# An encoder layer on one core: the first weights' fetch, two weight sums and one mean put elsewhere in the order

## The chip, the cores and the metric

The kernel runs on one core of a Trainium2 chip. The metric is the device time of one launch in microseconds (us). The engines are PE (TensorE: matmuls and transposes; PEld is its weight load), DVE (VectorE), ACT (ScalarE), POOL (GpSimd) and SP (SyncE, which here only issues DMA transfers). ACT and POOL also have DMA queues of their own. A line number such as L844 is a line of the kernel before.

## The reference

One encoder layer over x (1024 tokens, width 1024) with a conditioning vector c. It has three residual sub-layers, each `x <- LayerNorm(ALPHA * x + w * gate(c) * f(x * (1 + scale(c)) + shift(c)))`: a SwiGLU feed-forward network with a hidden width of 2816, a mixer (half convolution with 31 taps, half differential attention with 4 heads of two softmax maps each), and a second feed-forward network. Scale, shift and gate are products of silu(c) with a matrix of 1024 x 9216.

```python
def swiglu(h, w_in, w_out):
    gate, up = jnp.split(h @ w_in, 2, axis=-1)
    return (jax.nn.silu(gate) * up) @ w_out
```

## The kernel before, in words

Every fp32 operand is split into a rounded part and its remainder (`split`, L142: the cast on ACT at L143, the subtraction on DVE at L144), and a product takes three matmuls: high x high, high x low, low x high. The feed-forward networks multiply by a Strassen-like scheme with seven products: weights and activations are cut in quarters, and sums of quarters are formed on DVE (`in_sums`, L359, for the weights; the `t` tiles in `mid` for the activations).

The input phase of a feed-forward network works on 22 pairs j of column strips, one gate and one up strip each. `in_load` (L336) fetches a pair's raw weights in four transfers of 256 KB, `in_gate` (L352) splits the gate's quarters into `ah` and `al`, and `in_sums` forms four sums (L364 to L366, L368) and splits them into `sh` and `sl`.

The startup of the first network is written out by hand in `early` (L818). It works through four blocks kk of 256 columns. `first_ada` (L756) and `first_x` (L767) issue the loads on SP. `first_mod` (L773) multiplies the conditioning matrix by silu(c), partly on DVE (L780, L782), partly on PE (L788), and joins the halves on PE (L798) and ACT (`part` at L795, B and A at L802). `first_h` transposes x on PE (L810), and ACT applies B and A (`h`, L280). The result is rounded on ACT (L845), and `right_lo` (L830) forms its remainder on DVE (L832). The first pair's raw weights are issued on ACT's queue at the very start; its gate split stands behind block 0, the first three sums and their split behind block 1, the fourth behind block 3.

`mid` (L859) then treats the second half of the tokens: `h`, the sums `t` (L876, L877) with their splits, and behind the first products the subtractions of L899 and L900. From there `in_steps` (L411) runs the pairs, and `hook(j)` (L945) puts other work between them: `mix_load` (L919) and `mix_part` (L925) fetch parts of the mixer's weights on POOL's DMA queue, two per pair, split them and store them to a scratch in memory.

`out_phase` (L558) is the second half of a feed-forward network: 7 x 11 steps, each with its `prep` (L572: loads on SP, splits) and 12 matmuls (L610); `evac` (L626) takes the results out. In the first network's output phase, between the steps, `sums_load` (L668) fetches pieces of the second network's weights on POOL's queue, and `sums_part` (L675) forms their sums, splits them and stores them (L686). There are eight such units, one every nine steps. The same stretch runs the layer norm of finished tokens (`rstd_of`, L240, a power on POOL at L244; `nm` at L259; the scaling on ACT at L260).

In the attention, `scores` (L1183) makes two score maps per step, with a row-max on DVE (L1196) and an exponential on ACT. Beside it `conv_flip` and `conv_stat` (L1308) do the convolution's layer norm over channels: variances, a power on POOL (L1313), the negative scaled means `nm` (L1317, DVE), a scaling on ACT (L1320). `conv_back` (L1323) transposes the result back.

The order on each engine is that of a planner, which starts from the order of the program. `tc.issue_after(x)` ties an instruction behind x, on x's own engine alone. `pace["V"]` and `pace["S"]` hold the latest marked instructions of DVE and ACT.

## Time and profile before

| | |
|---|---|
| median of 3 runs | 1866.86 us (1865.17 to 1867.88) |
| profiled execution | 1868.7 us |
| its span | 1866.9 us |
| PE busy | 97% |
| DVE busy | 77% |
| ACT busy | 42% |
| POOL busy | 17% |
| DMA, mean | 160 GB/s |

The span is what the profile's times count from, first instruction to last; the execution's own time is 1.8 us longer. Busy shares are over the whole span. A time in brackets at the end of a row is how long the engine was idle ahead of the instruction, and what it then waited for.

### The profile page before, as it was taken

The numbers are of one execution on the slowest core, as the hardware profiler recorded it, in microseconds if no ns is written. First come the engines' busy times: TensorE is split into PE (matmuls) and PEld (weight loads), VectorE is DVE, ScalarE is ACT, GpSimd is POOL, SyncE is SP. The second block draws the span as 40 slices with busy tenths as digits, with TensorE's granted clock in tenths as the row PEclk, the third lists the DMA queues.
The fourth block names the chain that finished last, engine by engine and source line by source line (L and its number), as shares of the span: only waits on it lengthen the run. The fifth ranks groups of instructions, "written<-read, shape, count | busy, mean of one in ns | idle before, by whom it ended". The sixth has DMA issues, their size and how long they took to land.

```text
span 1866.9 us, 23501 instructions
## 1 busy us (share of the span) xinstructions
PE 1808.8 (97%) x8538; PEld 1499.9 (80%) x8538; DVE 1440.4 (77%) x2029; ACT 784.7 (42%) x1296; POOL 308.7 (17%) x336
## 2 busy tenths in 40 slices
PE   4999999999999999999999999999999999999997
PEld 4788888887888877888888888878888888888886
DVE  6988787898699788899876676587775766569888
ACT  3633333333455543112167783363333333354540
POOL 0001010011211122026658650100000000000011
PEclk9999999999999999999999999999999999999999
DMA  9378777775895423322100027145553443187432
GB/s 318 105 232 289 248 236 232 248 266 185 290 360 178 147 68 119 107 68 78 59 1 1 24 91 248 70 143 188 174 177 119 138 131 127 52 300 273 130 119 74
DMA packets 223602, 299.22 MB, mean 160 GB/s; under 512 B 16618, under 2 KB 127327, under 8 KB 223486
## 3 DMA queue, kind: packets, MB, share of 16 engines
q1 hardware_dynamic: 207018, 249.44, 41.2%
q0 software_dynamic: 13120, 45.10, 6.8%
q10 hardware_dynamic: 3348, 3.18, 0.5%
q8 instruction: 67, 1.10, 0.2%
q14 instruction: 49, 0.40, 0.1%
HBM read 215.35 MB, written 82.31 MB: 159 GB/s over the span
## 4 chain that ended last, share of the span: by engine, by line
PE 70%; DVE 12%; DMA 6%; ACT 4%; POOL 3%; issue 3%; SPq 1%; POOLq 0%; DVEq 0%; ACTq 0%
PE fo L610 16%; PE glu L1046 4%; PE mo L1428 4%; PE vp L1093 2%; PE kp L1093 2%; ACT p L1198 2%; PE fi_4A L396 1%; PE fi_9A L396 1%; PE fi_6A L396 1%; PE fi_14A L396 1%; PE fi_10A L396 1%; PE fi_16A L396 1%; PE fi_11A L396 1%; PE fi_8A L396 1%; PE qp L1093 1%
## 5 line engine op out<-in xcount | busy, mean ns | idle before, releaser
L610 PE MATMUL fo<-wr,gl 128*128 128x512 f32 x1848 | 422.3, 390 | 3.9 <-DVE pv L653 2.5
L610 PEld LDWEIGHTS fo<-wr,gl 128*128 128x128 f32 x1848 | 346.2, 188 | 78.0 <-DVE pv L653 3.7
L1065 DVE SCALAR_TENSOR_TENSOR cacc<-u,convw,cacc 128x1012 f32<-128x1012 f32 (+14 forms) x120 | 151.0, 1325 | 0.2
L144 DVE TENSOR_TENSOR gl<-gr,gl 128x512 fp32r<-128x512 f32 x148 | 101.9, 694 | 11.6 <-ACT gl L143 10.1
L143 ACT CAST gl<-gr 128x512 fp32r<-128x512 f32 x148 | 90.9, 618 | 31.3 <-DMA gr<-gd 25.4
L144 DVE TENSOR_TENSOR sl<-sf,sh 128x1024 fp32r<-128x1024 f32 x40 | 49.0, 1224 | 65.0 <-ACT sh L143 64.9
L1196 DVE TENSOR_REDUCE mx<-sc 128x1 f32<-128x1024 f32 x64 | 75.5, 1216 | 25.4 <-PE sc L1194 25.3
L1198 ACT ACTIVATE p<-sc,mx 128x1024 f32<-128x1024 f32 x64 | 71.3, 1115 | 35.7 <-DVE mx L1196 35.6
L143 ACT CAST sh<-sf 128x1024 fp32r<-128x1024 f32 x40 | 42.2, 1054 | 103.0 <-issue 7.9
L156 DVE SCALAR_TENSOR_TENSOR ada<-adaw,c_act,ada 128x512 f32<-128x512 f32 x98 | 73.3, 748 | 13.1 <-DMA adaw<-in_w_ada_dram 12.8
L418 POOL DMA_DIRECT2D gd<-gf x8 | 4.3, 542 | 430.9 <-DVE gf L484 429.7
L244 POOL TENSOR_TENSOR rr<-rv,mhalf 128x1 f32<-128x1 f32 x24 | 22.1, 920 | 290.7 <-DVE rv L242 290.6
L446 ACT ACTIVATE gf<-gf 128x512 f32<-128x512 f32 x44 | 27.8, 633 | 96.4 <-DVE gf L445 96.3
L466 ACT ACTIVATE gf<-gf 128x512 f32<-128x512 f32 x44 | 27.7, 629 | 96.2 <-DVE gf L465 96.2
L143 ACT CAST wr<-wa 128x512 fp32r<-128x512 f32 x66 | 41.1, 623 | 59.3 <-PE fo L610 55.6
L144 DVE TENSOR_TENSOR sl<-r,sh 128x1024 fp32r<-128x1024 f32 x44 | 53.6, 1222 | 16.0 <-ACT sh L143 15.7
L1046 PE MATMUL glu<-hm,gluh 128*128 128x512 f32 x256 | 65.6, 392 | 0.0
L1247 POOL TENSOR_TENSOR p<-p,p 128x1024 f32<-128x1024 f32 x27 | 64.2, 2376 | 1.5
L143 ACT CAST wr<-wb 128x512 fp32r<-128x512 f32 x66 | 40.1, 620 | 56.5 <-PE fo L610 36.7
L1264 PE MATMUL av<-vf,aT 128*128 128x128 f32 x512 | 62.4, 276 | 0.8 <-ACT cacc L1327 0.8
L144 DVE TENSOR_TENSOR wr<-wa,wr 128x512 fp32r<-128x512 f32 x66 | 45.5, 690 | 19.9 <-ACT wr L143 19.9
L1264 PEld LDWEIGHTS av<-vf,aT 128*128 128x128 f32 x512 | 59.8, 192 | 1.3 <-ACT cacc L1327 1.1
(3439 smaller groups left out, 4853.2 us busy)
## 6 DMA issues: line engine op xcount, KB each, us to landing
gr<-gd SPq DMA_DIRECT2D x148, 256.0 KB
adaw<-in_w_ada_dram SPq DMA_DIRECT2D x56, 512.0 KB
gd<-gf SPq DMA_DIRECT2D x102, 256.0 KB
r<-in_ffn_w_in_dram SPq DMA_DIRECT2D x84, 256.0 KB
ra<-in_ffn_w_in_dram SPq DMA_DIRECT2D x66, 256.0 KB
mwi<-mw POOLq DMA_DIRECT2D x24, 512.0 KB, 5.5
wb<-in_ffn_w_out_dram SPq DMA_DIRECT2D x44, 256.0 KB
wa<-in_ffn_w_out_dram SPq DMA_DIRECT2D x44, 256.0 KB
```

The source lines that it names most:

```text
L143: a = S.copy(hi, x)
L144: b = eng.tensor_tensor(lo, x, hi.bitcast(F32), ALU.subtract)
L156: V.scalar_tensor_tensor(acc, raw[:, jj], c_act[:, n : n + 1], acc, ALU.mult, ALU.add)
L396: pe_last[:] = [PE.matmul(ps, lhsT=w[:, k], rhs=x, start=k == 0 and n == 0 and not more, stop=k == 3 and n == 2, skip_group_check=more,).ins]
L610: PE.matmul(ps, lhsT=g[:, x, ts_], rhs=w[:, y], start=n in (1, 2, 3) and k == i == 0, stop=k == NK - 1 and i == 2, skip_group_check=n not ...
L1046: PE.matmul(q[2 * m + h], lhsT=w[:, m * P : (m + 1) * P], rhs=hm[k][h][:, x], start=k == 0 and n == 0, stop=k == KD - 1 and n == 2,)
L1065: V.scalar_tensor_tensor(acc[:, lo_t:hi_t], u[:, lo_t + sh : hi_t + sh], convw[:, i, jj : jj + 1], acc[:, lo_t:hi_t], ALU.mult, ALU.add,)
L1093: PE.matmul(pss[t], lhsT=hk[:, x, ts_], rhs=w, start=k == 0 and n == 0, stop=k == KD - 1 and n == 2)
L1196: V.tensor_reduce(mx_, ps, axis=AX.X, op=ALU.max, negate=True)
L1198: S.activation(pe, ps, AF.Exp, bias=mx_, accum_out=sm[:, e : e + 1])
L1264: PE.matmul(ps[:, 0:P], lhsT=aT[:, kt], rhs=vf[kt][:, h * P : (h + 1) * P], start=kt == 0, stop=kt == 7)
L1428: pe = PE.matmul(ps, lhsT=x[:, ts_], rhs=w[:, ds_], start=n == 0, stop=n == total - 1)
```

## The change

Four edits. In `early`, the first pair's raw weights are issued behind the second block's rounding on ACT, and the gate split, the four sums and their splits stand behind the last block. In `mid`, the subtractions of L899 and L900 stand behind the last remainder of the `t` tiles. Two of the eight weight sums leave the output phase and are done by `mix_load` and `mix_part` as the last two units, behind the 40 units of the mixer's weights. In the attention, `nm` of `conv_stat` stands behind the latest row-max.

```diff
@@ out_phase
-            if s == 0 and i < 72:
-                if i % 9 == 2:
-                    ms = sums_load(i // 36, i // 9 % 4)
-                elif i % 9 == 8:
-                    sums_part(ms, i // 36, i // 9 % 4)
+            if s == 0 and i < 54:
+                n_, at = divmod(i, 9)
+                if at == 2:
+                    ms = sums_load(*divmod(n_ + 2, 4))
+                elif at == 8:
+                    sums_part(ms, *divmod(n_ + 2, 4))
@@ early
-            with tc.issue_after(c_silu.ins):
-                raws = [in_load(wp, s, w_in, 0, S)]
+            raws = [None]
...
                     rounded = S.copy(hi[kk], hb[kk]).ins
+                if kk == 1:
+                    with tc.issue_after(rounded):
+                        raws[0] = in_load(wp, s, w_in, 0, S)
                 with tc.issue_after(summed):
                     if kk:
                         right_lo(kk - 1)
-                    if kk == 0:
+                    if kk == 3:
                         L[0].update(in_gate(wp, s, 0, raws[0]))
-                    elif kk == 1:
-                        in_sums(wp, s, 0, raws[0], L[0], order=(0,))
-                    elif kk == 3:
-                        right_lo(3)
-                        in_sums(wp, s, 0, raws[0], L[0], order=(1,))
+                        ra, rb, r4 = raws[0]
+                        V.tensor_tensor(ra[:, 2], rb, ra[:, 2], ALU.add)
+                        V.tensor_tensor(rb, ra[:, 0], rb, ALU.subtract)
+                        V.tensor_tensor(ra[:, 0], ra[:, 2], ra[:, 0], ALU.subtract)
+                        V.tensor_tensor(ra[:, 1], ra[:, 1], ra[:, 0], ALU.subtract)
+                        for i in range(2):
+                            sh = wp.tile([P, 2, 4, P], F32R, tag="sh", bufs=3, name=f"sh{s}_0_{i}")
+                            sl = wp.tile([P, 2, 4, P], F32R, tag="sl", bufs=3, name=f"sl{s}_0_{i}")
+                            with tc.issue_after(rounded):
+                                split(sh, sl, r4[:, i::2])
+                            L[0].update({f"S{2 * i + 2 - e}": (sh[:, e], sl[:, e]) for e in range(2)})
+                            if i == 0:
+                                right_lo(3)
@@ mid
+            ready = rest
             for kk in range(5):
                 if kk < 4:
                     b, h, t = hb[kk], hc[kk], t12[kk]
-                    right_b22(f"r0_{kk}", ops, h)
-                    V.tensor_tensor(h[:, 0], h[:, 1], h[:, 0], ALU.subtract)
-                    V.tensor_tensor(h[:, 1], b[:, 1], t[:, 1], ALU.subtract)
+                    with tc.issue_after(ready):
+                        right_b22(f"r0_{kk}", ops, h)
+                        V.tensor_tensor(h[:, 0], h[:, 1], h[:, 0], ALU.subtract)
+                        V.tensor_tensor(h[:, 1], b[:, 1], t[:, 1], ALU.subtract)
@@ mix_load, mix_part, units
+            if isinstance(src, tuple):
+                r = t[:, 0].rearrange("p (s n) -> p s n", s=4)
+                for dst, x in zip((r[:, 0::3], r[:, 1:3]), src):
+                    G.dma_start(dst, x)
+            else:
+                G.dma_start(t[:, 0], src)
...
-                if hs:
+                if hs and hs[0] is None:
+                    sums_of(t[:, 0].rearrange("p (s n) -> p s n", s=4))
+                elif hs:
...
+            if hs and hs[0] is None:
+                for x in range(2):
+                    G.dma_start(dst[:, x], t[:, x].rearrange("p (s n) -> p s n", s=4))
+            else:
+                G.dma_start(dst, t)
...
+        w2 = a["ffn2_w_in"][0].rearrange("(k e p) (s n) -> k e p s n", e=2, p=P, s=2)
+        for k in range(2):
+            units.append((tuple(w2[k, e][:, :, 0:P] for e in range(2)), mws[0][:, :, :, k], None))
@@ scores
-                V.tensor_reduce(mx_, ps, axis=AX.X, op=ALU.max, negate=True)
+                pace["V"] = V.tensor_reduce(mx_, ps, axis=AX.X, op=ALU.max, negate=True).ins
@@ conv_stat
-            V.scalar_tensor_tensor(nm, mv[:, :, 0], -1.0, r, ALU.mult, ALU.mult)
+            with tc.issue_after(pace["V"]):
+                V.scalar_tensor_tensor(nm, mv[:, :, 0], -1.0, r, ALU.mult, ALU.mult)
```

`sums_of` holds the same four sums as L679 to L682.

## Rows read from the trace of the kernel before

**Rows 1.** The page's first part: busy us, share, instructions of each engine.
```profile
PE 1808.8 (97%) x8538; PEld 1499.9 (80%) x8538; DVE 1440.4 (77%) x2029; ACT 784.7 (42%) x1296; POOL 308.7 (17%) x336
```

**Rows 2.** Stretches: length, busy PE, PEld, DVE, ACT, POOL, PE's clock, DMA share, GB/s.
```profile
14.00:40.00 26.00, 16.51 (x75) 15.66 (x75) 19.25 (x25) 11.09 (x33) 0.00 (x0) 1.00 1.09 347
50.00:67.00 17.00, 17.00 (x86) 14.00 (x85) 16.89 (x22) 13.98 (x19) 0.00 (x0) 1.00 0.22 62
67.00:83.00 16.00, 14.17 (x58) 9.98 (x57) 15.34 (x21) 9.91 (x13) 0.00 (x0) 1.00 0.20 64
1056.00:1060.00 4.00, 3.62 (x14) 2.95 (x15) 1.51 (x5) 4.00 (x11) 2.68 (x2) 0.50 0.00 0
```

**Rows 3.** The chain of waits up to 85 us: start, length, what.
```profile
20.63 6.76 DMA ada<-in_w_ada_dram
...
27.41 6.76 DMA ada<-in_w_ada_dram
...
41.22 5.67 DMA xc<-in_x_dram
```

**Rows 4.** Timeline of the DMA triggers on ACT's and SP's queues, startup.
```profile
3.13 6.83 ACTq L349 DMA_DIRECT2D r<-in_ffn_w_in_dram  x3
...
35.11 6.07 SPq L349 DMA_DIRECT2D r<-in_ffn_w_in_dram  x4
...
52.03 2.02 SPq L349 DMA_DIRECT2D r<-in_ffn_w_in_dram  x4
```

**Rows 5.** Timeline of ACT, startup.
```profile
15.42 1.47 ACT L143 CAST ah<-r 128x1536 fp32r<-128x1536 f32 x1 [12.50 <-DMA r<-in_ffn_w_in_dram]
...
29.92 1.05 ACT L143 CAST sh<-r 128x1024 fp32r<-128x1024 f32 x1
30.86 1.06 ACT L845 CAST r_1bh<-h 128x1024 fp32r<-128x1024 f32 x1
31.80 0.73 ACT L795 ACTIVATE part<-ada0q,bada 128x1 f32<-128x1 f32 x4
39.36 0.41 ACT L802 ACTIVATE B<-ada0p,part 128x1 f32<-128x1 f32 x2 [6.83 <-PE ada0p L798]
...
39.96 1.46 ACT L280 ACTIVATE h<-hT,B,A 128x512 f32<-128x512 f32 x2
```

**Rows 6.** Timeline of DVE, startup.
```profile
16.92 1.76 DVE L144 TENSOR_TENSOR al<-r,ah 128x1536 fp32r<-128x1536 f32 x1 [1.43 <-ACT ah L143]
...
25.24 0.69 DVE L366 TENSOR_TENSOR r<-r 128x512 f32<-128x512 f32 x1
...
49.59 1.23 DVE L832 TENSOR_TENSOR r_3bl<-h,r_3bh 128x1024 fp32r<-128x1024 f32 x1 [4.25 <-ACT r_3bh L845]
50.73 1.22 DVE L144 TENSOR_TENSOR sl<-r,sh 128x1024 fp32r<-128x1024 f32 x1
```

**Rows 7.** Timeline of the first output phase, 660 to 692 us, all engines.
```profile
662.84 0.77 POOL L686 DMA_DIRECT2D mws<-ms  x1 [2.29 <-issue]
...
664.23 0.21 DVE L259 TENSOR_SCALAR nm<-mv,rr 128x1 f32<-128x1 f32 x1 [2.82 <-POOL rr L244]
...
668.21 3.04 PE L610 MATMUL fo<-wr,gl 128*128 128x512 f32 x12 [1.55 <-DVE pv L653]
...
683.10 0.29 DVE L680 TENSOR_TENSOR ms<-ms 128x128 f32<-128x128 f32 x1
...
689.65 2.59 PE L610 MATMUL fo<-wr,gl 128*128 128x512 f32 x10 [0.93 <-DVE wr L144]
```

**Rows 8.** Timeline of DVE, 498 to 512 us.
```profile
504.24 0.69 DVE L144 TENSOR_TENSOR wr<-wb,wr 128x512 fp32r<-128x512 f32 x1 [2.49 <-ACT wr L143]
```

**Rows 9.** Timeline of the attention: DVE and PE at 1053 to 1117 us.
```profile
1052.90 0.16 DVE L1317 SCALAR_TENSOR_TENSOR cnm<-cmv,cr 128x4 f32<-128x4 f32 x1 [4.37 <-POOL cr L1313]
...
1055.98 0.73 PE L1178 MATMUL qTl<-ident_r,ql 128*128 128x128 f32 x4 [2.34 <-DVE aT L1256]
...
1116.87 1.91 PE L276 MATMUL cB<-ident,cacc 128*128 128x128 f32 x16
```

More of the change, by code (lines that the diff above doesn't have):

```diff
@@ L921, in mix_load, with sums_of @@
             t = wp.tile([P, 2, H], F32, tag="mw", bufs=2, name="mw")
-            G.dma_start(t[:, 0], src)
-            loaded.append((t, *rest))
+            if isinstance(src, tuple):
[4 more added lines that the diff above has]
+                G.dma_start(t[:, 0], src)
+            loaded.append((t, *rest))
+        def sums_of(r):
+            V.tensor_tensor(r[:, 2], r[:, 3], r[:, 2], ALU.add)
+            V.tensor_tensor(r[:, 3], r[:, 0], r[:, 3], ALU.subtract)
+            V.tensor_tensor(r[:, 0], r[:, 2], r[:, 0], ALU.subtract)
+            V.tensor_tensor(r[:, 1], r[:, 1], r[:, 0], ALU.subtract)
         def mix_part():
@@ L932, in mix_part @@
                 V.tensor_tensor(t[:, 0].bitcast(F32R), t[:, 0], t[:, 1], ALU.subtract)
-            G.dma_start(dst, t)
+            if hs and hs[0] is None:
[3 more added lines that the diff above has]
+                G.dma_start(dst, t)
         units = []
```

## The prediction, made before the changed kernel ran

> **What bounds the kernel now.** I read the page's list of engines first: PE is busy for 97% of the 1866.9 us [rows 1], so all that an edit can win are the few stretches in which PE stands or runs at half clock; an edit that fills idle time of another engine is worth nothing. The table by stretches then gives the stages. Startup, 14 to 40 us: the DMA engines are full (share 1.09, 347 GB/s) while DVE has 19.25 of 26 us and ACT 11.09. At 50 to 67 us, where the first pair's products run, DVE has 16.89 of 17 us and PE 17.00; at 67 to 83 DVE has 15.34 of 16 and PE only 14.17 [rows 2]. So until 83 us DVE is nearly solid: what comes late on DVE at 50 us comes late for PE too. The chain of waits up to 85 us shows why the startup lasts as long as it does: transfer after transfer, each link beginning where the one before ended (20.63 + 6.76 = 27.39, then 27.41) [rows 3]. Between two links lie eight transfers in the order of the program, those of SP and ACT counted together: I read it as eight counters used in turn, where a transfer is issued only when the one eight before it has landed. That reading carries my largest term.
>
> **Part 1, the first pair's raw weights (`early`).** Removed from the start: four transfers of 256 KB, 1.05 MB, which at 347 GB/s [rows 2] held up all later ones by 3.0 us. They now stand on ACT behind the second block's rounding, in program order behind all 46 others of the startup.
>
> When does ACT get there? That rounding is at 30.86 for 1.06 us [rows 5], so 31.92; it is 3.0 earlier by the bytes, and the first `sh` cast (1.05, at 29.92 [rows 5]) no longer stands ahead of it: 27.9.
>
> When may it issue? Before, the block transfer whose link begins at 27.41 lands at 34.17 [rows 3]. Behind it are five more of these (1.31 MB), three x pieces (0.52 MB each) and the second pair's four raw pieces; at that rate they land at 37.9, then 39.4, 40.9, 42.4, then 43.2, 43.9. After the change all is 3.0 earlier. The eight counters make the moved four wait for the last two x pieces and the first two raw ones: 37.9, 39.4, 40.2, and about 42 for the last, which by then shares the engines. ACT executes in order, so it stands at its triggers from 27.9 to about 42.4. The last lands a link later, 5.67 by the shortest late link [rows 3]: 47.4 (a link is 5.67 to 6.76).
>
> What is queued behind ACT's triggers: the third block's `part` (0.73 [rows 5]), its B, A and `h` (39.36 to 41.42, 2.1 [rows 5]). From 42.4 that gives 45.2. Then the gate cast `ah`, which now needs the landing: 47.4 + 1.47 [rows 5] = 48.9; third rounding 49.9; fourth `part` 0.7, B, A, `h` 2.1, rounding 1.06: 53.8. DVE: third remainder 51.1, `al` 1.76, sums 4 x 0.69, fourth remainder 1.23 and two `sl` of 1.22 less their overlap [rows 6]: 52.9, 55.6, 56.8, 58.5. Before, DVE was through with the second `sl` at 51.95 [rows 6]. So it is 6.5 late, and in a stage where DVE is solid PE is late by about as much; PE's 1.83 us of idle time at 67 to 83 [rows 2] takes back perhaps 0.5. **Part 1: +6.0.** Lower end +4.3, if `ah` stands behind the fourth `part`; upper end +8.7, if it stands ahead of the third block's B; and a gain of 3.5 if ACT isn't held at all (first rival). The gate's and sums' work itself (1.76 + 4 x 0.69 + 2 x 1.22 = 7.0 us of DVE) used to lie in DVE's 6.75 us of idle time at 14 to 40 us; that cover is gone, which is why it shows.
>
> A page sentence, apart: the Trainium skill, page *DMA: Bandwidth & Descriptors*, section *Issuing engines are not separate DMA queues*, says that triggering DMAs from several engines changes only the time of the triggering sequencer, which is usually small. By it, ACT would pay little for four triggers and the total would be the first rival's; against it stand the 6.83 us that ACT's queue spent on three triggers of the same pieces at the start [rows 4].
>
> **Part 2, the subtractions in `mid`.** They are put behind the last rounding of the sums on DVE; nothing is added. DVE is solid there [rows 2], so order alone changes nothing but who is served first: 0. Bounds: a gain of 1.0 if the T1 operands come sooner and PE's idle time at 67 to 83 shrinks, a loss of 0.5 if the B22 operands come late.
>
> **Part 3, two of the eight weight sums.** They leave the first output phase and go to the end of the first input phase, on POOL's DMA queue. In the output phase POOL triggers a store of the sums at 662.84 for 0.77; behind it stands the layer norm's power, so DVE's `nm` comes at 664.23 after 2.82 idle, ACT's `x` and the next weight rounding follow, and PE waits 1.55 at 668.21 and, behind the last unit's DVE and ACT work, 0.93 at 689.65 [rows 7]. Both late units vanish from there: 2.48 less a little for the next one late (the gate weights' own cast). Taken: **-2.3**. Bounds -3.0 and +1.0. What is added: twice four short sums of 0.29 [rows 7] and a split with 0.69 on DVE [rows 8], 3.7 us of DVE in all, two casts on ACT, four loads and four stores of POOL's queue, at about 500 to 507 us. DVE has there a gap of 2.49 ahead of 504.24 [rows 8], and PE doesn't wait for it. Cost 0; if that cover fails, the weight rounding at 504.24 is late by up to 2 us, of which +1.0 stands in the bound.
>
> **Part 4, the means' tie (`conv_stat`).** `nm` used to sit on DVE waiting for POOL's power: 4.37 us until 1052.90. The row-maxes behind it start only then, PE stands for 2.34 until 1055.98 [rows 9], and the stretch 1056 to 1060 runs at a granted clock of 0.50, the 1.2 GHz level, with 3.62 us of PE work that takes half as long at the full level [rows 2]. Tied behind the latest row-max, `nm` no longer blocks them. Gain: the 2.34 whole, and a third of the other 1.8, since DVE is what PE waits for there in any case: **-3.0**. Bounds 0 (the wait for POOL's power stays and merely comes after) and -4.1. New wait: the four scalings on ACT that need `nm` come some microseconds later; their results are read only in the transposes back, at 1116.87 [rows 9], 60 us on.
>
> **Sum:** +6.0 + 0 - 2.3 - 3.0 = +0.7. The profiled execution took 1868.7 us (span 1866.9, 1.8 outside it), 1.8 over the median of 1866.86. So 1869.4 for such an execution, **1867.6** for the median.
>
> **Rivals.** *First: ACT isn't held.* If the moved transfers have counters of their own, ACT pays only the triggers. SP needed 2.02 us for four such pieces with the queues quiet, 6.07 with them full [rows 4]. ACT is free at 30 to 34, the pieces land at 36 to 40, `ah` follows, and DVE is through with the second `sl` at 47.4 to 51: -0.9 to -4.5, taken -3.5. Total -8.8, **1858.1**. For it: 3.0 us of bytes really leave the front. Against it: the links [rows 3] begin on each other's ends to 0.02 us. Chance 0.24.
>
> *Second, the slower side: the landing decides.* If ACT's order has `ah` ahead of the third block's B, A and `h`, all these (2.1) wait for the landing as well, and the last transfer needs the long link, 6.76 [rows 3]: landing 48.8. `ah` 50.3, `h` 52.4, rounding 53.4, fourth block 57.3, DVE through with the second `sl` at 62, 10.1 late, part 1 = +9.6, total +4.3, **1871.2**. It decides as soon as the landing is later than ACT's release at 42.4, so it hangs on the order alone. For it: the cast of the first sums stands ahead of a rounding in ACT's row at 29.92 [rows 5], so this order puts casts early. Against it: that one stood behind its block's `h`. Chance 0.22.
>
> *Third: the parts 3 and 4 give nothing* (the waits are taken over by the next one late): part of the bounds above, +5 on the forecast; inside the slower chance.
>
> **Numbers.** The forecast (ACT held, `ah` behind `h`) has 0.54; its own range, from the bounds of the parts, is 1864.5 to 1870.5. Over all cases 1857 to 1873 leaves out about 2 in 10. A measurement of this kernel can tell about 0.2%, 3.7 us. Faster by more: the first rival, 0.24, and 0.08 from the forecast's lower bounds: 0.32. Slower: 0.15 of the second rival, whose time lies just beyond that bound, and 0.08 from the upper bounds of the forecast: 0.23. Between: 0.45.
>
> **What would show it.** Part 1: a gap of some 14 us in ACT's row after the second rounding, ended by DMA triggers, and `sl`'s second instance at about 58.5 instead of 50.73; it is wrong if ACT's third `part` starts by 35. Part 3: no `ms` store between 655 and 690, PE's waits at 668 and 689 gone, and nothing new at 500 to 510. Part 4: row-maxes at once where 4.37 stood, no stretch at clock 0.50 at 1056. Comparing the start of a late product in each trace gives the parts' sums one by one: +6.0 from 85 us on, +3.7 from 700 us on, +0.7 from 1070 on.

## The result, and the profile after

The changed kernel takes 1881.84 us (median of 4 runs, 1880.09 to 1882.63) against 1866.36 us for the kernel before: a ratio of 1.0082, 95% interval 1.0070 to 1.0093, some 15 us slower. The forecast was 1867.6 with a range up to 1873.0. PE runs the same 8538 matmuls and is busy for 1810.0 against 1808.8 us [rows 1] in a span that is 13.9 us longer (1880.8 us), so nearly all of the loss is time in which PE stood; the rest fits time at the lower clock, at which a matmul takes longer. The page's first part, after:

```profile
PE 1810.0 (96%) x8538; PEld 1501.0 (80%) x8538; DVE 1445.8 (77%) x2029; ACT 785.1 (42%) x1296; POOL 308.4 (16%) x336
```

Where does it arise? I matched each matmul of one trace with the same matmul of the other (same tiles, same shape, same place among its like) and took the difference of their starts. The medians by stretch, times of the kernel before:

| stretch, us | late by, us | what lies between |
|---|---|---|
| 95 to 115 | +13.3 | parts 1 and 2: startup |
| 140 to 180 | +13.75 | |
| 470 to 492 | +11.75 | |
| 505 to 560 | +23.6 | part 3: the two units, new place |
| 600 to 655 | +23.6 | |
| 700 to 740 | +19.8 | part 3: the two units, old place |
| 1000 to 1040 | +19.8 | |
| 1095 to 1100 | +11.3 | part 4 |
| 1130 to 1200 | +15.1 | part 4, given back |
| 1300 to the end | +13.9 | |

The steps without a part beside them, -2.0 before 492 us and -1.2 near 1280, are found in 13 and in 14 of the 15 kernels below too, with 0.6 to 2.4 and 0.4 to 1.8 us: for the larger share they probably belong to the one profiled execution of the kernel before, which was 1.8 us above its median. That is argued, not shown.

So the changed kernel lost 13.75 us in the startup, where +6.0 was forecast, and 12 us near 500 us, where 0 was forecast; the two gains came and were somewhat larger than forecast (3.7 for 2.3, 4.7 for 3.0).

**The startup.** ACT's timeline, changed kernel (start, length, engine, line, operation; in brackets how long ACT was idle and what it waited for):

```profile
26.20 1.04 ACT L845 CAST r_1bh<-h 128x1024 fp32r<-128x1024 f32 x1
37.09 3.71 ACTq L349 DMA_DIRECT2D r<-in_ffn_w_in_dram  x4
40.85 0.72 ACT L796 ACTIVATE part<-ada0q,bada 128x1 f32<-128x1 f32 x4 [13.61 <-DMA r<-in_ffn_w_in_dram]
48.76 1.47 ACT L143 CAST ah<-r 128x1536 fp32r<-128x1536 f32 x1 [7.19 <-DMA r<-in_ffn_w_in_dram]
50.13 0.41 ACT L803 ACTIVATE B<-ada0p,part 128x1 f32<-128x1 f32 x2
...
55.85 1.04 ACT L845 CAST r_3bh<-h 128x1024 fp32r<-128x1024 f32 x1
...
59.48 1.99 ACT L143 CAST sh<-r 128x1024 fp32r<-128x1024 f32 x2
```

ACT stands for 13.61 us at the four triggers, from 27.2 to 40.85, and then for 7.19 more until the last raw piece lands. `ah` is ahead of the third block's B: the third block's B, A and `h` and the whole fourth block come behind the landing. [rows 5] had the third block's B at 39.36. The chain of waits names the two links into which the triggers fall:

```profile
32.67 7.73 DMA r<-in_ffn_w_in_dram
...
40.43 8.30 DMA r<-in_ffn_w_in_dram
```

The second link ends at 48.73, so the landing is 1.3 us later than the 47.4 of the forecast. DVE's timeline, changed kernel:

```profile
50.26 1.76 DVE L144 TENSOR_TENSOR al<-r,ah 128x1536 fp32r<-128x1536 f32 x1 [15.22 <-ACT ah L143]
...
56.93 1.23 DVE L832 TENSOR_TENSOR r_3bl<-h,r_3bh 128x1024 fp32r<-128x1024 f32 x1 [1.81 <-ACT r_3bh L845]
58.07 0.68 DVE L857 TENSOR_TENSOR r<-r 128x512 f32<-128x512 f32 x1
58.95 0.69 DVE L887 TENSOR_TENSOR t<-h,h 128x512 f32<-128x512 f32 x1 [0.20 <-ACT h L280]
59.56 0.68 DVE L858 TENSOR_TENSOR r<-r 128x512 f32<-128x512 f32 x1
60.16 0.69 DVE L888 TENSOR_TENSOR t<-h,t 128x512 f32<-128x512 f32 x1
60.77 2.35 DVE L144 TENSOR_TENSOR sl<-r,sh 128x1024 fp32r<-128x1024 f32 x2
...
74.06 1.23 DVE L144 TENSOR_TENSOR r_2t1l<-t,r_2t1h 128x1024 fp32r<-128x1024 f32 x1 [2.21 <-ACT r_2t1h L143]
```

DVE stands for 15.22 us ahead of `al`, and is through with the second `sl` at 63.1 where it was 51.95 before [rows 6]. Behind the fourth block's remainder (56.93) it still has two of the four sums and two additions of the second tokens' `t` to do ahead of the `sl`. The stretches that answer to [rows 2]:

```profile
50.00:67.00 17.00, 13.20 (x59) 9.75 (x60) 14.05 (x16) 15.69 (x31) 0.00 (x0) 0.98 0.16 45
67.00:83.00 16.00, 14.87 (x59) 11.47 (x58) 13.58 (x19) 10.08 (x14) 0.00 (x0) 0.92 0.07 20
```

PE was full at 50 to 67 and is no longer, DVE has 2.4 to 3.0 us of idle time in each stretch, and the mean granted clock is below 1.00: behind a wait of PE's of 1.52 us that ends at 66.31 it is at 0.50, the 1.2 GHz level, for 3.4 us.

```profile
66.31:69.70 3.39, 3.39 (x8) 2.71 (x9) 3.29 (x4) 3.39 (x5) 0.00 (x0) 0.50 0.49 136
```

**Near 500 us.** All engines, changed kernel, 501 to 519 us:

```profile
506.01 1.15 POOL L964 DMA_DIRECT2D mwo<-mw  x2
509.66 2.27 POOL L938 DMA_DIRECT2D mw<-in_ffn_w_in_dram  x3 [2.50 <-DMA mwo<-mw]
...
513.31 0.29 DVE L945 TENSOR_TENSOR mw<-mw 128x128 f32<-128x128 f32 x1 [7.11 <-DMA mw<-in_ffn_w_in_dram]
...
518.77 11.46 PE L610 MATMUL fo<-wr,gl 128*128 128x512 f32 x39 [9.35 <-ACT gl L143]
```

POOL stores the last two units of the mixer's weights at 506, waits for these stores to land, loads the moved units into the same two buffers, and DVE stands 7.11 us for them; ACT's and DVE's next splits of the output phase are in order behind, and PE stands for 9.35 us. Behind this wait PE works at a granted clock of 0.50 until 523.7:

```profile
518.77:523.70 4.93, 4.93 (x12) 3.74 (x13) 4.92 (x9) 3.69 (x7) 1.51 (x2) 0.50 0.68 206
```

At the full level these 4.93 us would be half as long (an estimate). The 2.5 us and the wait of 9.35 are the 11.85 us by which the table falls there.

### The profile page after: what moved, and what is told of

Read it like the earlier page. It is cut to its first block, busy times and chain, and to the rows that moved or that the text cites. A ratio compares the mean times of both kernels' runs of the same rounds, so it can differ in the third digit from the quotient of the medians.

```text
span 1880.8 us, 23502 instructions
## 1 busy us (share of the span) xinstructions
PE 1810.0 (96%) x8538; PEld 1501.0 (80%) x8538; DVE 1445.8 (77%) x2029; ACT 785.1 (42%) x1296; POOL 308.4 (16%) x336
## 4 chain that ended last, share of the span: by engine, by line
PE 75%; DVE 10%; DMA 5%; ACT 4%; POOL 3%; issue 2%; SPq 1%; POOLq 0%; DVEq 0%; ACTq 0%
PE fo L610 19%; PE glu L1080 4%; PE mo L1463 4%; PE vp L1127 2%; PE kp L1127 2%; ACT p L1232 2%; PE fi_4A L396 1%; PE fi_9A L396 1%; PE fi_2A L396 1%; PE fi_3A L396 1%; PE fi_14A L396 1%; PE fi_6A L396 1%; PE fi_10A L396 1%; PE fi_16A L396 1%; PE fi_8A L396 1%
## 5 line engine op out<-in xcount | busy, mean ns | idle before, releaser
L610 PE MATMUL fo<-wr,gl 128*128 128x512 f32 x1848 | 424.2, 391 | 10.3 <-ACT gl L143 9.4
L144 DVE TENSOR_TENSOR gl<-gr,gl 128x512 fp32r<-128x512 f32 x148 | 103.0, 702 | 11.5 <-ACT gl L143 10.2
L143 ACT CAST sh<-sf 128x1024 fp32r<-128x1024 f32 x40 | 42.1, 1053 | 103.1 <-issue 11.9
L143 ACT CAST wr<-wa 128x512 fp32r<-128x512 f32 x66 | 41.1, 623 | 55.2 <-PE fo L610 52.4
L144 DVE TENSOR_TENSOR wr<-wa,wr 128x512 fp32r<-128x512 f32 x66 | 45.6, 691 | 19.8 <-ACT wr L143 19.7
```

The costliest lines, as they stand in the source:

```text
L143: a = S.copy(hi, x)
L144: b = eng.tensor_tensor(lo, x, hi.bitcast(F32), ALU.subtract)
L610: PE.matmul(ps, lhsT=g[:, x, ts_], rhs=w[:, y], start=n in (1, 2, 3) and k == i == 0, stop=k == NK - 1 and i == 2, skip_group_check=n not ...
```

## The experiments

Each of them is timed against the kernel before on the same chip, with 2 (e15_fetch_mid) to 11 runs; "late by" is the matching of the table above.

| kernel | median, us | ratio | interval | late at 95-115 | 140-180 | 505-560 | 600-655 | 700-740 | 1130-1200 |
|---|---|---|---|---|---|---|---|---|---|
| e1_fetch | 1878.04 | 1.0057 | 1.0040-1.0073 | 10.2 | 10.2 | 9.3 | 9.3 | 9.3 | 8.2 |
| e2_sums | 1875.03 | 1.0038 | 1.0023-1.0053 | -0.3 | 1.2 | 11.2 | 11.2 | 7.5 | 7.6 |
| e3_tie | 1863.81 | 0.9982 | 0.9972-0.9991 | -0.5 | 1.1 | 0.1 | 0.2 | 0.3 | -2.7 |
| e4_mid | 1868.16 | 1.0005 | 0.9995-1.0014 | 1.2 | 1.7 | 2.3 | 2.3 | 2.4 | 2.6 |
| e5_ahlast | 1875.26 | 1.0039 | 1.0025-1.0053 | 9.3 | 9.8 | 7.2 | 7.2 | 7.3 | 7.5 |
| e6_order | 1871.63 | 1.0026 | 1.0015-1.0037 | 5.9 | 6.3 | 4.4 | 4.4 | 4.4 | 3.4 |
| e7_sp_ahlast | 1876.67 | 1.0045 | 1.0029-1.0061 | 8.9 | 9.6 | 8.1 | 8.1 | 8.2 | 7.0 |
| e8_before | 1880.59 | 1.0068 | 1.0045-1.0091 | -0.3 | 0.8 | 16.5 | 16.5 | 12.7 | 11.5 |
| e9_slot | 1870.44 | 1.0018 | 1.0008-1.0028 | 0.7 | 0.7 | 1.0 | 7.1 | 3.3 | 3.5 |
| e10_defer | 1873.79 | 1.0041 | 1.0027-1.0056 | -0.4 | -0.2 | 0.8 | 8.8 | 5.0 | 5.3 |
| e11_defer_tie | 1868.62 | 1.0008 | 0.9996-1.0020 | -0.2 | -0.2 | -1.0 | 8.1 | 4.3 | 1.3 |
| e12_dense_tie | 1868.87 | 1.0008 | 0.9999-1.0017 | 0.0 | 1.4 | -0.5 | 9.7 | 6.0 | 1.3 |
| e13_no_mid | 1879.00 | 1.0068 | 1.0052-1.0084 | 10.0 | 10.7 | 20.0 | 20.0 | 16.3 | 11.6 |
| e15_fetch_mid | 1878.84 | 1.0065 | 1.0045-1.0084 | 11.9 | 12.3 | 11.7 | 11.8 | 11.7 | 10.8 |
| e14_tie_cl28 | 1860.98 | 0.9970 | 0.9958-0.9981 | 0.6 | 1.9 | 0.6 | 0.6 | 0.6 | -6.4 |

The eight kernels whose startup wasn't changed stand between -0.5 and 0.7 at 95 to 115 us and between -0.2 and 1.9 at 140 to 180: in a single trace, differences under about 1 us at the first place and 2 us at the second mean little. The clock is one cause of such scatter. e3_tie, e5_ahlast, e9_slot, e10_defer and e11_defer_tie each have 3.4 us at a granted clock of 0.50 near 870 us, where none of them changes anything, and are 1.5 to 1.7 us later behind it.

### The four parts by themselves

**e1_fetch**, the two hunks in `early` alone:

```diff
-            with tc.issue_after(c_silu.ins):
-                raws = [in_load(wp, s, w_in, 0, S)]
+            raws = [None]
...
+                if kk == 1:
+                    with tc.issue_after(rounded):
+                        raws[0] = in_load(wp, s, w_in, 0, S)
```

> Part 1 alone (the first pair's raw weights and sums; mid as before). In the trace of the full change the products stand 13.75 us later from 95 us on, with parts 1 and 2 both at work there. Theory (the held ACT and the late landing make all of it): +12 to +14, and the products from 120 us on are 13 to 14 late. Rival (part 2 costs some of it, since its subtractions no longer fill DVE's waits): +10.5 to +11.5 here and the rest in the run of part 2 or of both. Both expect ACT to stand at the four triggers until about 40.8 and the last raw piece to land at about 48.7.

It is 10.2 us late from 95 us on, 10.3 by the medians: a little under the rival's 10.5. So part 1 doesn't make all of the 13.75; ACT's row is that of the full change, with 13.59 us at the triggers and `ah` at 49.01.

**e4_mid**, the hunk in `mid` alone:

```diff
+            ready = rest
...
-                    right_b22(f"r0_{kk}", ops, h)
+                    with tc.issue_after(ready):
+                        right_b22(f"r0_{kk}", ops, h)
```

> Part 2 alone, the subtractions behind the last remainder of the t tiles. Theory (DVE is solid at 50 to 67 us, so order alone changes nothing): -1.0 to +0.5. Rival (the subtractions used to fill DVE's waits for ACT, and come late as work of their own now): +1 to +3, with DVE idle at 60 to 66 us where it was solid.

1.2 to 1.7 us late in the startup, hardly more than kernels with the old startup show there, and not to be told from the kernel before by its time (1.0005). It doesn't gain, and alone it loses little or nothing.

**e2_sums**, the hunks in `out_phase`, `mix_load`, `mix_part` and the list of units alone:

```diff
-            if s == 0 and i < 72:
+            if s == 0 and i < 54:
...
+        for k in range(2):
+            units.append((tuple(w2[k, e][:, :, 0:P] for e in range(2)), mws[0][:, :, :, k], None))
```

> Part 3 alone. In the trace of the full change the products fall back by 12.0 us at 496 to 501 us (11.6 to 23.6) and win 3.7 back at 660 to 700. Theory (the two units stand in a chain at the end of the mixer's weights: the store of the unit before, the load into its buffer, the sums, and ACT's next weight split behind them in order): +12 - 3.7 = +8.3, with a PE wait of 9 to 10 us near 505. Rival (the long wait arises only with the startup late, since the queues are shifted against each other): -2 to -4.

The wait is there without any change in the startup, PE's timeline:

```profile
507.10 13.25 PE L610 MATMUL fo<-wr,gl 128*128 128x512 f32 x50 [9.43 <-ACT gl L143]
```

0.0 late at 470 to 492, 11.2 at 505, 7.5 at 700: a fall of 11.2 (the wait, and 1.7 for the 3.4 us at a clock of 0.50 behind it) and a gain of 3.7, as the theory had it; the time is 7.3 us above that of the kernel before. The rival, a shift of the queues by the late startup, is out.

**e3_tie**, the hunks in `scores` and `conv_stat` alone:

```diff
-                V.tensor_reduce(mx_, ps, axis=AX.X, op=ALU.max, negate=True)
+                pace["V"] = V.tensor_reduce(mx_, ps, axis=AX.X, op=ALU.max, negate=True).ins
...
-            V.scalar_tensor_tensor(nm, mv[:, :, 0], -1.0, r, ALU.mult, ALU.mult)
+            with tc.issue_after(pace["V"]):
+                V.scalar_tensor_tensor(nm, mv[:, :, 0], -1.0, r, ALU.mult, ALU.mult)
```

> Part 4 alone. In the trace of the full change the products gain 8.5 us at 1052 to 1100 and lose 3.8 at 1102 to 1115, net -4.7. Theory (DVE no longer stands for POOL's power; nothing else hangs on it): -4.5 to -5, median near 1862. Rival (most of it is slack that the late startup left elsewhere): 0 to -2.

4.7 us by the trace (1.9 late at 1000 to 1040, 2.7 ahead from 1130 on), 4.0 by the medians. The tie gains by itself.

### What makes the startup late

**e5_ahlast**: part 1, with `ah` behind the fourth block's rounding.

```diff
-                        L[0].update(in_gate(wp, s, 0, raws[0]))
+                        with tc.issue_after(rounded):
+                            L[0].update(in_gate(wp, s, 0, raws[0]))
```

> Part 1 alone, with the gate cast ah tied behind the fourth block's rounding on ACT. In the run of part 1 alone the products are 10.2 us late from 95 us on. Landing of the last raw piece as there, about 48.7, and ACT held at its triggers until about 40.8. Theory (ah ahead of the third block's B, A and h makes these wait for the landing as well): B, A, h of both blocks and both roundings pass between 41 and 48.6, ah at 48.7, products late by 4.5 to 7. Rival (the late landing alone decides, whatever stands behind it): still 9 to 10.5.

**e7_sp_ahlast**: the same, with SP as the trigger.

```diff
-                        raws[0] = in_load(wp, s, w_in, 0, S)
+                        raws[0] = in_load(wp, s, w_in, 0)
```

> As e5_ahlast, with the four transfers triggered by SP, behind its own last ones, instead of ACT. Theory (both count: ACT's standing at its triggers, and the landing): ACT no longer stands, the fourth rounding is done before 42, the landing is still at 46 to 49, ah right behind it, products late by 2 to 4.5, less than in e5_ahlast. Rival (once ah is last, only the landing counts): the same as e5_ahlast within 0.7.

ACT's timeline of e5_ahlast:

```profile
47.10 1.04 ACT L844 CAST r_3bh<-h 128x1024 fp32r<-128x1024 f32 x1
50.27 1.47 ACT L143 CAST ah<-r 128x1536 fp32r<-128x1536 f32 x1 [2.12 <-DMA r<-in_ffn_w_in_dram]
57.77 1.05 ACT L143 CAST sh<-r 128x1024 fp32r<-128x1024 f32 x1
58.71 1.48 ACT L143 CAST ah<-r 128x1536 fp32r<-128x1536 f32 x1
60.10 1.04 ACT L143 CAST sh<-r 128x1024 fp32r<-128x1024 f32 x1
```

From PE's and DVE's timelines of e5_ahlast, and PE's stretch behind the third row (busy times and clock as in [rows 2]):

```profile
51.79 0.80 PE L396 MATMUL fi_0A<-r_0bh,ah 128*128 128x512 f32 x1 [2.69 <-ACT ah L143]
59.63 0.69 DVE L445 TENSOR_TENSOR gf<-fi_0A,p 128x512 f32<-128x512 f32 x1 [1.28 <-PE fi_0A L396]
65.44 0.80 PE L396 MATMUL fi_1A<-r_0bh,al 128*128 128x512 f32 x1 [1.61 <-DVE al L144]
65.44:68.70 3.26, 3.26 (x8) 2.58 (x9) 3.26 (x5) 0.00 (x0) 0.00 (x0) 0.50 0.98 279
```

And ACT's of e7_sp_ahlast:

```profile
41.26 1.04 ACT L844 CAST r_3bh<-h 128x1024 fp32r<-128x1024 f32 x1
50.04 1.47 ACT L143 CAST ah<-r 128x1536 fp32r<-128x1536 f32 x1 [7.73 <-DMA r<-in_ffn_w_in_dram]
```

The fourth rounding starts at 56.11 in e1_fetch, at 47.10 and at 41.26 here, and the products are 10.2, 9.3 and 8.9 late. Both times the rival's number came out. Whether ACT stands 13.6 us at its triggers or not is worth 0.4 us at most (by the medians e7_sp_ahlast is the slower of the two). The order of `ah` is worth about 1 us at 95 us, but more is hidden: the landing is later here (50.2 and 50.0 instead of 49.0), and in both kernels the clock falls to 0.50 for 3.4 us near 65 us, which it doesn't in e1_fetch. That is up to 1.7 us of their lateness; what the order would be worth with the same clock isn't shown. Behind the landing both kernels are alike. The first product needs `ah`, and starts at 51.8 and 51.6 where it started at 45.39 before. On DVE the second tokens' `t` stand between the sums, and the first product's combination (L445, which waits for PE) and a remainder of `t` stand ahead of the two `sl`. The sums' casts on ACT are not what holds them: in e5_ahlast the first ends at 58.8, and its `sl` starts at 60.23, right behind L445; the second `sl` ends at 63.7. The Trainium skill, page *DMA: Bandwidth & Descriptors*, section *Issuing engines are not separate DMA queues*, says that all DMAs run on the same 16 DMA engines whichever engine starts them, and that starting them on several saves only the sequencer's time. For the total these two runs agree with it (9.3 and 8.9 late), though ACT's 13.6 us at the triggers were real.

**e6_order**: part 1, with the same transfers on SP in the same order, but written behind the moved four.

```diff
-            xc = [first_x(kk, 1) for kk in range(2)]
-            raws.append(in_load(wp, s, w_in, 1))
-            xc.extend(first_x(kk, 1) for kk in range(2, 4))
+            xc = []
...
                         raws[0] = in_load(wp, s, w_in, 0, S)
+                    xc.extend(first_x(n, 1) for n in range(2))
+                    raws.append(in_load(wp, s, w_in, 1))
+                    xc.extend(first_x(n, 1) for n in range(2, 4))
```

> Part 1 alone, with SP's last six kinds of transfers (the second tokens' x pieces and the second pair's raw weights) written behind the moved four, so that SP issues the same transfers in the same order but the moved four have lower numbers in the program. Theory (eight counters in turn in the order of the program, each transfer issued only when the one eight before has landed): the four wait for the fourth block's modulation weights, ACT is free at about 33 instead of 40.8, the last piece lands at about 40 instead of 48.7, and the products are late by 0 to 3 instead of 10.2. Rival (ACT's triggers wait because the engines are full, whatever the numbers): ACT free at 38 or later, landing later than 46, products still 8 to 10 late.

ACT's timeline of e6_order:

```profile
35.45 0.72 ACT L795 ACTIVATE part<-ada0q,bada 128x1 f32<-128x1 f32 x4 [7.26 <-DMA ada<-in_w_ada_dram]
44.76 1.47 ACT L143 CAST ah<-r 128x1536 fp32r<-128x1536 f32 x1 [8.59 <-DMA r<-in_ffn_w_in_dram]
```

ACT is free at 35.45 instead of 41.1, and what ended its wait is a landing of the modulation weights. Only the number in the program differs, so the counters by number are borne out; the triggers are not merely slow because the engines are full. The landing comes at 44.7, 4.3 us earlier than in e1_fetch (a smaller step than the theory's 8.7), and the products are 5.9 to 6.3 late instead of 10.2: 4.1 earlier, and more than the 0 to 3 late that the theory had. ACT's order is the same in both, and in neither does the granted clock fall between 56 and 100 us. **In this pair the lateness follows the landing one to one.**

**e13_no_mid** and **e15_fetch_mid**: the full change without the hunk in `mid`, and the hunks of `early` and `mid` alone. Their edit is the hunk of e4_mid, left out of the one and joined to e1_fetch in the other.

> The full change without part 2 (the subtractions in mid stay where they were). Part 1 alone was 10.2 late at 95 us, part 2 alone 1.2 to 1.7, the full change 13.3 to 13.75. Theory (part 2 costs about 1.5 alone and some 3.5 behind a late landing, since DVE then waits for ACT with the subtractions held back): 10 to 10.5 late at 95 us, median 3 to 4 under the full change, near 1878. Rival (the parts just add up with scatter; 13.75 is 10.2 + 1.5 + 2 of something else): 11.5 to 12.5 late, median 1.5 under.

> Parts 1 and 2 without 3 and 4. Theory (the startup's 13.75 us are made by these two together): 13 to 14 late at 95 us, and DVE idle for 2.2 us ahead of the third block's remainder as in the full change. Rival (something of parts 3 and 4 reaches back into the startup by the planner): under 12.5.

Without part 2 the full change is 10.0 late at 95 us instead of 13.3; with part 2, part 1 alone goes from 10.2 to 11.9. So part 2 costs 1.6 to 3.3 us behind a late landing: e13_no_mid comes out as its theory had it at 95 us, e15_fetch_mid as its rival, and it has 0.64 us of DVE idle where the full change has 2.21. The 1.4 us between the two are clock. In both, PE waits 1.5 us near 66 us; behind it the full change has 3.4 us at 0.50 (above), and e15_fetch_mid stays at the full level:

```profile
66.14:69.70 3.56, 3.56 (x16) 2.96 (x17) 3.46 (x4) 3.48 (x5) 0.00 (x0) 1.00 0.51 147
```

In stretches of about the same length, 8 matmuls run in the one and 16 in the other, and from there on the products of the two kernels differ by 1.5 to 1.7 us. Why the clock fell in one of them only, and whether it does so in every execution, isn't shown. A stretch of e13_no_mid, to be held against that of the full change above:

```profile
67.00:83.00 16.00, 14.86 (x62) 11.03 (x61) 15.89 (x21) 11.14 (x16) 0.00 (x0) 1.00 0.09 24
```

With the subtractions in their old place DVE has 15.89 us at 67 to 83, with the tie 13.58, and the granted clock stays at 1.00 instead of 0.92. The subtractions were what DVE did while it waited for ACT. Held back, they come later as work of their own: at the products of 80 to 87 us (times of the kernel before) both kernels with parts 1 and 2 lose another 2 us and more, e1_fetch and e13_no_mid nothing. A second stretch of 3.4 us at 0.50, from 93 us on in both, is part of it.

### What makes the fall near 500 us

**e8_before**: part 3, with the two sums ahead of the last two of the mixer's units.

```diff
-            units.append((tuple( ...
+            units.insert(38 + k, (tuple( ...
```

> Part 3 alone, with the two moved weight sums ahead of the last two of the mixer's units, so that two of the mixer's own units come last. In the run of part 3 alone the products fall back by 11.2 us at 495 to 501 and win 3.7 at 660 to 700. Theory (a 21st round of two units is what costs: store of the round before, landing, load into its buffer, landing, all on POOL's queue behind the last pair's stores, with ACT and DVE in order behind it; whose data it is doesn't matter): the same fall of 9 to 13 at the same place. Rival (the sums' small transfers and their four additions make it): a fall of 0 to 5.

The fall is there, at the same place, and with 17.3 us (0.8 ahead at 470, 16.5 late at 505) larger than any of the two expected; now POOL has four stores of sums in front of the last loads. So the 21st round costs this although the mixer's own units are in it; the sums' small stores add to it. PE's wait of 14.79 and 2.3 for a clock of 0.50 until 516.5 make the fall. POOL and PE:

```profile
502.88 0.75 POOL L950 DMA_DIRECT2D mws<-mw  x1 [2.27 <-issue]
503.63 0.56 POOL L928 DMA_DIRECT2D mw<-in_mix_w_out_dram  x1
```

```profile
511.82 18.35 PE L610 MATMUL fo<-wr,gl 128*128 128x512 f32 x70 [14.79 <-ACT gl L143]
```

**e9_slot**: part 3, the two units in buffers of their own.

```diff
-            t = wp.tile([P, 2, H], F32, tag="mw", bufs=2, name="mw")
+            t = slot(f"mws{len(units)}", dt=F32) if isinstance(src, tuple) else wp.tile([P, 2, H], F32, tag="mw", bufs=2, name="mw")
```

> Part 3 alone, with the two moved sums loaded into buffers of their own instead of the mixer weights' pair of buffers, so that their loads needn't wait for the stores of the units before and POOL issues them ahead of the last pair's stores. Theory (the chain store, landing, load, landing at the end of POOL's queue makes the fall): PE's wait of 9 to 10 us near 505 shrinks to 0 to 3, the products are -2.5 to +1 in the end. Rival (the sums' place in DVE's and ACT's order, ahead of the output phase's first splits, makes it): a wait of 5 us or more stays.

POOL's timeline, and PE's behind it:

```profile
480.92 1.45 POOL L926 DMA_DIRECT2D mws<-in_ffn_w_in_dram  x2
...
488.70 0.56 POOL L418 DMA_DIRECT2D gd<-gf  x1 [1.60 <-DVE gf L484]
...
493.98 1.21 POOL L952 DMA_DIRECT2D mwo<-mw  x2
```

```profile
541.50 18.86 PE L610 MATMUL fo<-wr,gl 128*128 128x512 f32 x81 [1.64 <-DVE wr L144]
```

The loads are issued from 480.92 on, ahead of the last pair's stores, and the fall shrinks from 11.2 to 1.3 us at 497. That the sums still stand in DVE's and ACT's order ahead of the output phase's splits costs these 1.3 us at most. The chain through the two shared buffers is shown as the cause. But the kernel isn't faster, as the theory had it: 6 us are lost at 537 to 540 and at 610, where neither the kernel before nor e2_sums loses anything.

**e10_defer**: as e9_slot, the units' work at two steps of the output phase.

```diff
+            if s == 0 and i in (5, 14):
+                later.pop(0)()
             if s == 0 and i < 54:
...
             while loaded:
-                mix_part()
+                if j == NJ:
+                    later.append(mix_part)
```

> As e9_slot, and the sums, splits and stores of the two units wait until the 6th and the 15th step of the output phase. Theory of the chain: with the loads early it makes no more difference, within 1.5 us of e9_slot. Rival (their place in DVE's and ACT's order counts): better than e9_slot by 2 us or more. Both: the 3.7 us won at 660 to 700 stay, so -2 to -4 against the kernel before if nothing falls back at 500.

Neither expectation holds: by the medians it is 6.9 us slower than the kernel before, e9_slot 3.5. Nothing is lost at 500, and 8 us are lost at 546 to 553 and at 610; the second of these is part of what e9_slot loses too. **e11_defer_tie** (with the tie) and **e12_dense_tie** (the tie, and all eight units in the output phase, closer together) were tries at a version that keeps both gains. The second's edit:

```diff
-            if s == 0 and i < 72:
-                if i % 9 == 2:
-                    ms = sums_load(i // 36, i // 9 % 4)
+            if s == 0 and i < 56:
+                n_, at = divmod(i, 7)
+                if at == 1:
+                    ms = sums_load(*divmod(n_, 4))
```

> e10_defer with part 4 (the means' tie), without parts 1 and 2. If both gains stand side by side: -2 to -4 from the sums and -4 from the tie, -6 to -8, median near 1860. If the sums' gain is eaten up by the new work at the 6th and 15th step: the tie alone, -3 to -4.

> Part 4 with all eight weight sums left in the output phase, one every seven steps instead of every nine, so that the last is through at step 55 instead of 71 and none stands beside the layer norm at 660 to 700; without parts 1 to 3. If those two units' place, not their number, cost PE the 3.7 us there: -6 to -8, median near 1860. If the denser units cost PE elsewhere: -3 to -4, as with part 4 alone, with new PE waits between 560 and 650.

Both miss: 1.0008, no faster than before and slower than the tie alone. The 3.7 us at 660 to 700 are won, and 9 to 10 us are lost at 540 to 615, as the columns 505-560 and 600-655 of the table show. PE's longest new wait in e9_slot at that place is behind ACT's evacuation of a product, in PE's timeline:

```profile
613.78 16.41 PE L610 MATMUL fo<-wr,gl 128*128 128x512 f32 x64 [2.20 <-ACT pu L629]
```

The clock is at 0.50 for 3.4 us behind it, which makes 3.9 us of the 2.20. Why the same place falls in all four is not settled. The planner writes every engine's order anew for each kernel, and the evacuation stands behind more splits; that was not tried by itself.

### What the tie gives back, and a faster version

**e14_tie_cl28**: the tie, and two more of the attention's steps combined on DVE.

```diff
-CL = 30
+CL = 28
```

> Part 4 with the constant CL at 28 instead of 30, so that the steps 28 and 29 of the attention combine their two maps on DVE in one instruction (1.28 us) instead of on POOL in two (1.1 and 2.4). Part 4 alone was 6.5 us ahead at 1095 us and gave 3.8 back by 1115, where a combine on DVE took 3.23 instead of 1.28 beside POOL's 2.37 us addition. Theory (POOL's late combines, and DVE's beside them, make what is given back): 2 to 4 of it stays, median 1860 to 1862. Rival (the attention's end is bound by the chain of row-max, exponential and transposes anyway): within 1 of part 4 alone.

e3_tie is 6.5 ahead at 1095 us and 2.7 ahead at 1130. What stands between, on POOL, DVE and PE:

```profile
1103.88 2.37 POOL L1247 TENSOR_TENSOR p<-p,p 128x1024 f32<-128x1024 f32 x1
1104.10 3.23 DVE L1244 SCALAR_TENSOR_TENSOR p<-p,c,p 128x1024 f32<-128x1024 f32 x1
...
1106.31 1.09 PE L276 MATMUL aT<-ident,p 128*128 128x128 f32 x8 [1.01 <-POOL p L1247]
```

With CL at 28 these steps no longer use POOL, in DVE's timeline:

```profile
1101.35 1.28 DVE L1244 SCALAR_TENSOR_TENSOR p<-p,c,p 128x1024 f32<-128x1024 f32 x1
```

7.8 ahead at 1095 and still 6.4 ahead at 1130; 1860.98 us, a ratio of 0.9970 (0.9958 to 0.9981). That is as the theory had it: 1.4 us are given back instead of 3.8. It is the fastest of all kernels here, 5 us faster than the kernel before, and nothing of parts 1 to 3 is in it. By the times alone it can't be told from e3_tie, since the two intervals overlap; that CL adds to the tie rests on the traces.

## Why the prediction was wrong

**Part 1, +6.0 forecast, 10.2 measured.** The mechanism was right: the eight counters, ACT standing at its triggers (to 40.85, forecast 42.4), the late landing (48.7, forecast 47.4), and a solid DVE that hands the lateness to PE. The last link was taken as 5.67, that of an x piece, where the chain of before has one of the very pieces that are moved, not among the rows shown:

```profile
6.19 8.49 DMA r<-in_ffn_w_in_dram
```

With it the landing would have been forecast at about 50.2, 1.5 us too late instead of 1.3 too early.

The step that failed is the one behind the landing, "fourth remainder 1.23 and two `sl` of 1.22 less their overlap [rows 6]: 52.9, 55.6, 56.8, 58.5". The changed kernel is through at 63.1, 4.6 us later. Of these, 3.1 come from ACT: the fourth rounding ends at 56.9 instead of 53.8, since the landing is 1.3 later and `ah` stands ahead of the third block's B, A and `h`, as the second rival had it. (With a landing at 48.8 and +9.6 for part 1 this rival was right in order and close in size.) The other 1.5 come from DVE: the forecast has 4.7 us from the fourth rounding to the end of the `sl`, for the rest of the sums, the fourth remainder and the two `sl`; the rows have 6.2, for the same and two additions of the second tokens' `t`, 1.2 us. The forecast's sum held only the first pair's own work.

The order was not all of it: with `ah` even behind the fourth rounding (e5_ahlast) the kernel is 9.3 to 9.8 late, up to 1.7 of it by the clock, because the first product itself starts with `ah` and the second tokens' work on DVE stands in between here too. ACT's standing was given weight that it doesn't have: without it (e7_sp_ahlast) next to nothing is won. The first rival, a gain of 3.5 if ACT isn't held, had the pieces land at 36 to 40. No run with part 1 has a landing before 44.7, and where ACT isn't held the kernel is still 9 us late.

**Part 2, 0 forecast, 1.2 to 1.7 alone (hardly more than the scatter of a trace), 1.6 to 3.3 with part 1.** The step that failed is "DVE is solid there [rows 2], so order alone changes nothing but who is served first: 0." It was read from the trace of before; with part 1 DVE is no longer solid, and work tied behind the last remainder is missing as a filler. Some 1.5 of the 3.3 are the fall of the clock at 66 us, which only one of the two kernels with both parts shows. The bound of +0.5 was taken for this part by itself, not in the state in which part 1 leaves the stage.

**Part 3, -2.3 forecast, +7.5 measured.** The gain was there, 3.7: 1.55 + 0.93 and a third wait of 0.47 beside them, none of which e2_sums has, and 0.8 that isn't traced to a wait. The term that failed is "Cost 0; ... of which +1.0 stands in the bound": the four loads and four stores were counted as POOL's work, and the gap on DVE as cover. What wasn't asked is what the load waits for. A 21st round in two buffers needs the 20th round's stores landed, and these stand behind the last pair's stores on POOL's queue. It cost 11.2 us when alone: 9.43 of waiting, and the rest by the clock behind the wait. The trace of before had the pattern, in POOL's timeline, where a mixer's load follows the landing of a store:

```profile
476.60 0.55 POOL L922 DMA_DIRECT2D mw<-in_mix_w_out_dram  x1 [2.58 <-DMA mwo<-mw]
```

**Part 4, -3.0 forecast, -4.7 in the trace, -4.0 by the medians.** Right in mechanism and place: the row-maxes of the changed kernel no longer wait for POOL,

```profile
1080.13 2.36 DVE L1230 TENSOR_REDUCE mx<-sc 128x1 f32<-128x1024 f32 x2
1082.40 0.86 DVE L1352 SCALAR_TENSOR_TENSOR cnm<-cmv,cr 128x4 f32<-128x4 f32 x1
```

and the 4.37 us of [rows 9] are gone. The size was taken too small by a third. The term that was mis-sized is "a third of the other 1.8": the stretch at the lower level is longer than the 4 us that were read, from 1056.0 to 1062.9 in the kernel before,

```profile
1056.00:1062.80 6.80, 6.42 (x24) 5.35 (x25) 3.67 (x6) 5.78 (x14) 3.50 (x2) 0.50 0.00 0
```

and e3_tie has the full level there. Half of 6.42 is 3.2 us; with the wait of 2.34 that is 5.5 of the 5.8 us that e3_tie has won by 1064 us. What POOL gives back at 1100 to 1115 was not seen.

**The sum.** 13.75 - 2.0 + 11.8 - 3.7 - 4.7 - 1.2 = 13.9 by the traces, against the +0.7 of the forecast: 7.75 of the 13.2 us between them lie in the startup and 10.4 in part 3, less 1.7 in part 4 and 3.2 that have no part beside them. The slower side had 0.23, and its rival's 1871.2 held only the startup's lateness. No case had part 3 as a loss of more than 1.0.

## What to carry to other kernels

A round more in a ring of buffers is not priced by its work but by the chain that it lengthens: store, landing, load, landing; look up what the load's buffer still holds, and what stands ahead of the store on its queue. A transfer that is moved behind others is priced by its landing and by everything that was ordered behind it on every engine, not by the engine that triggers it: with the order left alone, the end followed the landing one to one. Work of later stages that the planner has put in between belongs in the sum too. And when several parts act on one stage, cost the later ones in the state in which the first leaves it. A wait of PE's can cost more than its length: look at the granted clock behind it, which here added 1.7 to 3.2 us to waits of 1.5 to 14.8.

## What was not expected of the hardware

A DVE instruction with two inputs can stand still beside a POOL instruction with two inputs. The combine on DVE takes 1.28 us alone; in e3_tie, begun 0.22 us behind POOL's addition of 2.37 us, it takes 3.23: it ends at 1107.33, 1.08 us behind POOL's end at 1106.25. The small `cnm` of the changed kernel, 0.16 us in [rows 9], takes 0.86 beside POOL's addition, from 1082.40 on, and ends 0.02 us behind it:

```profile
1080.88 2.36 POOL L1281 TENSOR_TENSOR p<-p,p 128x1024 f32<-128x1024 f32 x1
```

The Trainium skill, page *SBUF — State Buffer*, section *SBUF: two separate sides*, states such an exclusive lock between DVE and GpSimd, for DVE operations with two inputs in SBUF against a GpSimd operation that reads SBUF; these rows agree with it.

And the granted clock of 1.00 in [rows 2] says little about the startup. In PE's timeline of the kernel before, the first products follow each other at 0.43 us from 46.39 to 48.09, and at 0.23 us from 52.11 on; the trace's first entry of the clock lies between the two, at 49.1. In the kernels with part 1 it lies at 51.8 to 56.1.
